# VectorE's chain of the stick-breaking branch, from the maximum on, in pieces of one head, each tied to a weight split

## The chip, the cores and the metric

One core of a Trainium2 chip runs the whole program; the other cores are idle. The metric is the time of one execution on the device in microseconds (us), and lower is better. TensorE (PE; its weight loads are PEld) does the matmuls, VectorE (DVE), ScalarE (ACT) and GpSimd (POOL) the rest, and SyncE (SP) issues nearly all loads. Each engine takes its instructions in the order in which the program lists them.

## The reference, cut to what matters

Two layers; in each, four token mixers (a, b, c, d) share one input projection, each has a gate, and a merge adds the four with per-channel gates. The change is in branch d, stick-breaking attention with 4 heads of 64 and a sequence of 512:

```python
z = jnp.einsum('bqhd,bkhd->bhqk', qblk, k).astype(jnp.float32) * scale
mask = kpos[None, :] < t[:, None]
log1m = jnp.where(mask, jax.nn.log_sigmoid(-z), 0.0)
after = lax.cumsum(log1m, axis=3, reverse=True) - log1m
a = jnp.where(mask, jnp.exp(jax.nn.log_sigmoid(z) + after), 0.0)
return jnp.einsum('bhqk,bkhd->bqhd', a.astype(v.dtype), v)
...
for i, y in enumerate((y_a, y_b, y_c, y_d)):
    gate = jax.nn.sigmoid(h @ w_merge[l, i] + b_merge[l, i])
    merged = merged + gate * (y @ w_branch[l, i])
```

## The kernel before

**Matmuls in three passes.** Every large product is made of three fp32r matmuls of 128x512 (`mm3`, L195 to L197): the high part of one operand with the high part of the other, high with low, and low with high. So each weight that is loaded must first be split.

**Weight chunks.** `split_chunk` loads one 128-column chunk of a weight into a `stage` buffer (three of them), ScalarE (L184) and GpSimd (L102) round its high part, and one VectorE subtraction (L186) makes the low part. The first matmul of a chunk waits for L186. High and low parts live in four buffers `w5`, that is two chunks, so the rounding of a chunk can begin only when TensorE has read the chunk before the last for the last time. A merge chunk (`merge_chunks`) has 24 matmuls on the shared input `hT` and 6 on a branch's output `y`; then ScalarE takes a Tanh (L395), VectorE multiplies and adds (L400, L402), and GpSimd accumulates (L403).

**Branch d.** Its 4 heads are worked in two chains of 2 heads, `pr` 0 and 1, in each layer: four chains in all. The scores of the four query blocks (128, 256, 384 and 512 wide) of both heads are packed into three tiles, `ze[0][0..2]`: the first two (tag `x4`) are 128 x 2 heads x 512, the third (tag `su`) 128 x 2 x 256. The first holds query block 3, the second blocks 1 and 2, the third block 0 and nothing else of weight. For the three tiles in turn VectorE takes min (L757) and ScalarE Exp and Ln(1+.) (L758, L761). Then, tile by tile, VectorE takes the maximum with z (L767), runs reversed prefix sums in place (L775, one scan for each query block and head), and subtracts (L776), and ScalarE takes Exp (L777). `pv_cluster` transposes the result (L332), copies it (L334) and multiplies it with v (L339); `finish_pair` (L347 to L349) applies the gate.

**What sets the order.** The program is written down once; a scheduler in the framework then orders the instructions of each engine by priorities and its own estimate of time. `high_priority` puts branch work ahead of the merge chunks around it, so that the chunks fill TensorE while a branch waits for its softmax. `after(first, then, ...)` adds a dependency by hand. Two of these concern the chain: each Ln waits for the rounding of a certain chunk (`w_round`), and the maximum of tiles 0 and 1 waits for the low part of a certain chunk (`w_split`), so that the split goes first on VectorE:

```python
larger = V.tensor_tensor(ze[1][j], ze[0][j], ze[1][j], op=OP.max)
if j < 2:
    after(w_split[(n_10 + 1, n_11 + 3)[pr] + j], larger, "weights first")
```

`n_10` and `n_11` are the numbers of the first chunk of two stretches of the merge. In the rows of the first layer, chain 0 runs beside the chunks `w_450/451`, `w_457/458` (that is `n_11`) and `w_463/464`, chain 1 beside `w_476/477`, `w_480/481`, `w_486/487` and the two after them, `w_710/711` and `w_716/717` (after the change the first number of a name is the same or a little higher in the later ones). The even or odd larger number of a pair is the low part, which L186 writes. At the end of branch c stand the chunks `w_809/810`, `w_815/816` and `w_823/824`.

Of the kernel before, what the change touches and what calls it, by code (L numbers as in the profile page):

```python
# [12 lines left out]
AF = mybir.ActivationFunctionType  # L13
OP = mybir.AluOpType
# [74 lines left out]
def hybrid_trunk(ctx: ExitStack, tc: tile.TileContext, x, norm_g, w_in, mla_q_norm, mla_w_uq, mla_kv_norm,  # L89
# [3 lines left out]
    V, A, G, T = nc.vector, nc.scalar, nc.gpsimd, nc.tensor  # L93
# [55 lines left out]
    def ps_o():  # L149
        return mk(ps, [P, 512], F32, "po", 1)  # L150
# [37 lines left out]
    def after(first, then, why):  # L188

        tc.add_manual_dep(then.ins, first.ins.name, mybir.DependencyInfo(  # L190
            mybir.DependencyClass.Sync, mybir.DependencyReason.DATA), reason=why)
# [49 lines left out]
    w_round, w_split = [], []  # L241
# [209 lines left out]
    for l in range(DEPTH):  # L451
# [274 lines left out]
        n_10 = len(w_split)  # L726
# [8 lines left out]
        n_11 = len(w_split)  # L735
# [5 lines left out]
        with tc.high_priority(offset=tc.cur_priority - mark):  # L741
            y[3] = new_y()
            for pr in range(2):
                ze = [(x4([P, 2, 512]), x4([P, 2, 512]), unit_tile().rearrange("p (h c) -> p h c", h=2)) for _ in range(2)]
                place = ((1, 384, 512), (2, 0, 256), (1, 0, 384), (0, 0, 512))

                def part(i, qt, h):
                    j, c0, c1 = place[qt]
                    return ze[i][j][:, h, c0:c1]

                for qt in (3, 2, 0, 1):
                    w = (qt + 1) * P
                    for h in range(2):
                        s = qk_unit(stacked(d_q[pr], d_k[pr][h], h), qt, w)
                        V.tensor_tensor(part(0, qt, h), s[:, :w], mask_tab[:, S + 1 - w:], op=OP.subtract)
                for j in range(3):
                    V.tensor_scalar(ze[1][j], ze[0][j], 30.0, None, op0=OP.min)  # L757
                    ex = A.activation(ze[1][j], ze[1][j], AF.Exp)  # L758
                with tc.issue_after(ex.ins):
                    for j in range(3):  # L760
                        ln = A.activation(ze[1][j], ze[1][j], AF.Ln, bias=1.0)  # L761

                        after(w_round[(n_10 + 1, n_11 + 2)[pr]], ln, "weights first")
                        if pr == 0:
                            after(ln, gelu, "one table at a time")
                for j in range(3):
                    larger = V.tensor_tensor(ze[1][j], ze[0][j], ze[1][j], op=OP.max)  # L767
                    if j < 2:

                        after(w_split[(n_10 + 1, n_11 + 3)[pr] + j], larger, "weights first")  # L770
                    for qt in range(NT):
                        if place[qt][0] == j:
                            for h in range(2):
                                er = part(1, qt, h)[:, ::-1]
                                V.tensor_tensor_scan(er, er, er, 0.0, op0=OP.add, op1=OP.bypass)  # L775
                    V.tensor_tensor(ze[0][j], ze[0][j], ze[1][j], op=OP.subtract)  # L776
                    A.activation(ze[0][j], ze[0][j], AF.Exp)  # L777
                acc = ps_o()
                for qts in ((3,), (2,), (0, 1)):
                    pv_cluster([([part(0, qt, h) for h in range(2)], qt,  # L780
                                 lambda h, kb: v_ad[1][:, kb, (2 * pr + h) * 64:(2 * pr + h + 1) * 64], False, True)
                                for qt in qts], acc)
                d_done = finish_pair(acc, gd, y[3], pr)
# [130 lines left out]
```

## Time and profile before

| | |
|---|---|
| median of 3 runs | 1095.86 us (1093.76 to 1097.98) |
| the profiled execution, its own time | 1093.13 us |
| its span, first to last instruction | 1091.4 us |
| TensorE busy in the span | 1068.1 us (98%) |
| VectorE / ScalarE / GpSimd busy | 592.9 us (54%) / 440.0 us (40%) / 251.4 us (23%) |
| granted TensorE clock, mean | 0.998 of full speed (2.4 GHz is 1) |

The span lies within the execution's own time; 1.7 us lie around it. A row of the timeline has the start in us from the span's start, the time that it takes, the engine, the source line and operation, output and inputs, and in brackets how long the engine was idle before and on what it waited. Several instructions of a line in a row are one row (x2, x8). The end of a matmul is modelled: matmuls of 128x512 follow each other some 0.23 us apart though each is listed with 0.39.

### The profile page before, as it was taken

How to read it: one execution, taken by the hardware profiler on the slowest of the kernel's cores; microseconds unless marked ns; L12 is line 12 of the kernel's file. 1: busy time of each engine (PE TensorE's matmuls, PEld its weight loads, DVE VectorE, ACT ScalarE, POOL GpSimd, SP SyncE). 2: the span in 40 equal slices, each digit the busy share in tenths (PEclk: the TensorE clock that was granted, in tenths of full speed). 3: DMA queues.
4: the chain of work that ended last, by engine and by line, in shares of the span. 5: the costliest groups of instructions: out<-in, count | busy, mean ns of one | idle time of the engine just before them, and what ended most of it. 6: DMA issues, size and time to landing. Idle time of an engine off the chain costs nothing.

```text
span 1091.4 us, 15131 instructions
## 1 busy us (share of the span) xinstructions
PE 1068.1 (98%) x5652; PEld 858.8 (79%) x5652; DVE 592.9 (54%) x1136; ACT 440.0 (40%) x894; POOL 251.4 (23%) x270
## 2 busy tenths in 40 slices
PE   8999999999999999999999999999999999999997
PEld 6888887877778878788888888778787888777886
DVE  6435565568645646355443565466857455563542
ACT  5424343454433535233243343434545334352322
POOL 3221020202133132342011311111023222323321
PEclk9999999999999999999999999999999999999999
DMA  8423252422232212246313323443132322213412
GB/s 249 105 58 78 65 152 64 141 73 78 73 87 82 74 54 68 87 124 191 103 39 98 79 77 88 117 126 102 44 97 75 95 73 68 78 49 113 139 58 77
DMA packets 161676, 100.86 MB, mean 92 GB/s; under 512 B 14913, under 2 KB 151489, under 8 KB 161602
## 3 DMA queue, kind: packets, MB, share of 16 engines
q1 hardware_dynamic: 160880, 98.75, 31.6%
q8 instruction: 44, 0.72, 0.3%
q10 hardware_dynamic: 722, 1.14, 0.3%
q14 instruction: 30, 0.25, 0.1%
HBM read 95.67 MB, written 4.19 MB: 92 GB/s over the span
## 4 chain that ended last, share of the span: by engine, by line
PE 88%; DVE 6%; DMA 2%; ACT 2%; issue 1%; SPq 0%; POOL 0%; POOLq 0%; DVEq 0%; ACTq 0%
PE pd L195 24%; PE pd L196 23%; PE pd L197 23%; PE po L339 5%; PE pss L302 4%; PE pt L332 4%; DMA stage<-in_w_out_dram 2%; DVE w L186 2%; DVE x L775 2%; PE pt L692 1%; ACT w L184 0%; DVE su L775 0%; DVE s L551 0%; DMA stage<-in_w_in_dram 0%; PE pd L643 0%
## 5 line engine op out<-in xcount | busy, mean ns | idle before, releaser
L195 PE MATMUL pd<-hT,w 128*128 128x512 f32 x832 | 333.7, 401 | 8.4 <-DVE w L186 8.2
L197 PE MATMUL pd<-hT,w 128*128 128x512 f32 x832 | 331.9, 399 | 0.0
L196 PE MATMUL pd<-hT,w 128*128 128x512 f32 x832 | 331.5, 398 | 0.0
L102 POOL TENSOR_SCALAR w<-stage 128x640 fp32r<-128x640 f32 (+1 forms) x104 | 72.3, 696 | 617.9 <-PE pd L196 316.6
L195 PEld LDWEIGHTS pd<-hT,w 128*128 128x128 f32 x832 | 156.5, 188 | 46.8 <-DVE w L186 11.5
L186 DVE TENSOR_TENSOR w<-stage,w 128x1280 fp32r<-128x1280 f32 (+1 forms) x104 | 145.4, 1398 | 83.5 <-ACT w L184 51.4
L197 PEld LDWEIGHTS pd<-hT,w 128*128 128x128 f32 x832 | 156.5, 188 | 35.2 <-issue 1.1
L196 PEld LDWEIGHTS pd<-hT,w 128*128 128x128 f32 x832 | 156.5, 188 | 33.4 <-issue 0.3
L403 POOL TENSOR_TENSOR s<-s,th 128x512 f32<-128x512 f32 x48 | 111.0, 2313 | 62.3 <-DVE th L402 59.2
L184 ACT ACTIVATE w<-stage 128x640 fp32r<-128x640 f32 x104 | 76.5, 736 | 88.8 <-PE pd L196 77.9
L314 ACT ACTIVATE su<-su,stat 128x128 f32<-128x128 f32 (+3 forms) x128 | 71.2, 557 | 76.5 <-DVE stat L312 76.4
L334 ACT ACTIVATE pt<-pt 128x384 f32<-128x384 f32 (+2 forms) x120 | 59.4, 521 | 96.0 <-PE pt L332 95.2
L395 ACT ACTIVATE th<-pd,bmT 128x512 f32<-128x512 f32 x64 | 43.9, 686 | 104.3 <-PE pd L197 104.0
L402 DVE SCALAR_TENSOR_TENSOR th<-th,pd 128x512 f32<-128x512 f32 x48 | 32.8, 684 | 75.1 <-PE pd L197 75.0
L332 PE MATMUL pt<-small,su 128*128 128x128 f32 x336 | 57.7, 279 | 1.5 <-DVE su L317 1.5
L195 PE MATMUL pd<-y,w 128*128 128x512 f32 x128 | 51.4, 404 | 0.3
L332 PEld LDWEIGHTS pt<-small,su 128*128 128x128 f32 x336 | 39.8, 140 | 14.4 <-issue 6.2
L197 PE MATMUL pd<-y,w 128*128 128x512 f32 x128 | 50.5, 395 | 0.0
L196 PE MATMUL pd<-y,w 128*128 128x512 f32 x128 | 50.4, 394 | 0.0
L312 DVE CUSTOM_DVE_ANT_0 su<-pss,dist_tab 128x128 f32<-128x128 f32 (+3 forms) x64 | 28.9, 486 | 37.8 <-PE pss L302 37.8
L196 PE MATMUL pd<-y,hT 128*128 128x512 f32 (+1 forms) x112 | 44.1, 397 | 0.0
L195 PE MATMUL pd<-y,hT 128*128 128x512 f32 (+1 forms) x112 | 43.4, 396 | 0.0
(251 smaller groups left out, 1540.6 us busy)
## 6 DMA issues: line engine op xcount, KB each, us to landing
stage<-in_w_merge_dram SPq DMA_DIRECT2D x64, 512.0 KB, 3.9
stage<-in_w_in_dram SPq DMA_DIRECT2D x38, 512.0 KB, 3.9
stage<-in_w_branch_dram SPq DMA_DIRECT2D x64, 128.0 KB, 3.8
stage<-in_w_out_dram SPq DMA_DIRECT2D x16, 512.0 KB, 4.1
stage<-in_w_in_dram SPq DMA_DIRECT2D x20, 256.0 KB, 3.8
x<-in_nsa_w_dram SPq DMA_DIRECT2D x8, 512.0 KB, 4.9
stage<-in_w_in_dram SPq DMA_DIRECT2D x8, 352.0 KB, 4.6
x<-in_tab_a_dram SPq DMA_DIRECT2D x4, 512.0 KB, 4.4
```

The source lines that it names most:

```text
L102: G.tensor_scalar(o, i, 1.0, 1.0, op0=OP.mult, op1=OP.mult)
L184: r = A.activation(hi[:, :a], src[:, :a], AF.Copy)
L186: return r, V.tensor_tensor(lo, src, hi.bitcast(F32), op=OP.subtract)
L195: first = T.matmul(acc, sh, mh, start=start, stop=False)
L196: T.matmul(acc, sh, ml, start=False, stop=False)
L197: T.matmul(acc, sl, mh, start=False, stop=stop)
L314: A.activation(e[:, :width], e[:, :width], AF.Exp, scale=-1.0, bias=st[:, 0:1], accum_out=st[:, 1:2])
L332: T.transpose(pt[:, i], u[0][h][:, kb * P:(kb + 1) * P], ident)
L334: ready = A.activation(pT[:, :n], pt[:, :n], AF.Copy)
L339: pv = T.matmul(acc[64 * h:64 * h + 64, qt * P:(qt + 1) * P], v(h, kb), pTs[h][:, i], start=(kb == 0 and not started), stop=(kb == qt and ...
L395: A.activation(th, pg, AF.Tanh, scale=0.5, bias=bmT[l][:, 8 * i + c:8 * i + c + 1])
L403: G.tensor_tensor(acc[:, j], acc[:, j], th, op=OP.add)
```

## The change

The loop over three tiles becomes a loop over five pieces: head 0 and head 1 of the first tile, head 0 and head 1 of the second, and the third tile whole. Each piece has its own maximum, its own scans (those of its query blocks and head), its own subtraction and its own Exp. Each maximum is tied to the split of a chunk: the pieces to the chunks 0, 1, 1, 2, 2 counted from `w_split[n_10 + 1]` in chain 0 and from `w_split[n_11 + 3]` in chain 1.

```diff
-                for j in range(3):
-                    larger = V.tensor_tensor(ze[1][j], ze[0][j], ze[1][j], op=OP.max)
-                    if j < 2:
-                        after(w_split[(n_10 + 1, n_11 + 3)[pr] + j], larger, "weights first")
+                for j, h, chunk in ((0, 0, 0), (0, 1, 1), (1, 0, 1), (1, 1, 2), (2, None, 2)):
+                    hs = slice(None) if h is None else h
+                    z, e = ze[0][j][:, hs], ze[1][j][:, hs]
+                    larger = V.tensor_tensor(e, z, e, op=OP.max)
+                    after(w_split[(n_10 + 1, n_11 + 3)[pr] + chunk], larger, "weights first")
                     for qt in range(NT):
                         if place[qt][0] == j:
-                            for h in range(2):
-                                er = part(1, qt, h)[:, ::-1]
+                            for h_ in range(2) if h is None else (h,):
+                                er = part(1, qt, h_)[:, ::-1]
                                 V.tensor_tensor_scan(er, er, er, 0.0, op0=OP.add, op1=OP.bypass)
-                    V.tensor_tensor(ze[0][j], ze[0][j], ze[1][j], op=OP.subtract)
-                    A.activation(ze[0][j], ze[0][j], AF.Exp)
+                    V.tensor_tensor(z, z, e, op=OP.subtract)
+                    A.activation(z, z, AF.Exp)
```

In the changed program the maximum is L770, the scan L776, the subtraction L777 and the Exp L778.

**First place: VectorE in chain 0** of the first layer, from the first maximum on (`x_493`, `x_494`, `su_2530` are z in the three tiles, `x_496`, `x_497`, `su_2533` the tiles that are summed). Before:

```order
L767 TENSOR_TENSOR x_496_2531<-x_493_2528,x_496_2531 128x1024
L767 TENSOR_TENSOR x_497_2532<-x_494_2529,x_497_2532 128x1024
L767 TENSOR_TENSOR su_2533<-su_2530,su_2533 128x512
L658 TENSOR_SCALAR gelu_2017<-gelu_2017 128x64
L775 SCALAR_TENSOR_TENSOR x_496_2531<-x_496_2531 128x512 x2
L775 SCALAR_TENSOR_TENSOR x_497_2532<-x_497_2532 128x128 x2
L775 SCALAR_TENSOR_TENSOR x_497_2532<-x_497_2532 128x384 x2
L775 SCALAR_TENSOR_TENSOR su_2533<-su_2533 128x256 x2
L659 TENSOR_TENSOR hid_1972<-gelu_2017,hid_1972 128x64
L400 SCALAR_TENSOR_TENSOR s_442_2189<-th_2266,pd_2268 128x512
L186 TENSOR_TENSOR w_464_2327<-stage_2323,w_463_2326 128x1280
```

Of the change, behind the two maxima of the first tile (one row, L770 x2):

```order
L770 TENSOR_TENSOR x_497_2532<-x_494_2529,x_497_2532 128x512
L776 SCALAR_TENSOR_TENSOR x_496_2531<-x_496_2531 128x512
L658 TENSOR_SCALAR gelu_2017<-gelu_2017 128x64
L776 SCALAR_TENSOR_TENSOR x_496_2531<-x_496_2531 128x512
L776 SCALAR_TENSOR_TENSOR x_497_2532<-x_497_2532 128x128
L776 SCALAR_TENSOR_TENSOR x_497_2532<-x_497_2532 128x384
L777 TENSOR_TENSOR x_493_2528<-x_493_2528,x_496_2531 128x512
L659 TENSOR_TENSOR hid_1972<-gelu_2017,hid_1972 128x64
L777 TENSOR_TENSOR x_493_2528<-x_493_2528,x_496_2531 128x512
L400 SCALAR_TENSOR_TENSOR s_442_2189<-th_2266,pd_2268 128x512
L777 TENSOR_TENSOR x_494_2529<-x_494_2529,x_497_2532 128x512
L186 TENSOR_TENSOR w_464_2327<-stage_2323,w_463_2326 128x1280
```

The second half of the second tile and the whole third tile (two maxima, four scans) now stand behind the split of `w_464`, and three subtractions of 512 columns stand ahead of it that stood behind.

**Second place: VectorE and ScalarE in chain 1** of the first layer (`x_521`, `x_522`, `su_2657` or `su_2663` are z; `x_524`, `x_525`, `su_2660` or `su_2666` the tiles that are summed). VectorE before:

```order
L402 SCALAR_TENSOR_TENSOR th_2471<-th_2471,pd_2473 128x512
L767 TENSOR_TENSOR x_524_2658<-x_521_2655,x_524_2658 128x1024
L767 TENSOR_TENSOR x_525_2659<-x_522_2656,x_525_2659 128x1024
L775 SCALAR_TENSOR_TENSOR x_524_2658<-x_524_2658 128x512 x2
L186 TENSOR_TENSOR w_711_3357<-stage_3353,w_710_3356 128x1280
```

VectorE in the change:

```order
L770 TENSOR_TENSOR x_524_2664<-x_521_2661,x_524_2664 128x512 x2
L776 SCALAR_TENSOR_TENSOR x_524_2664<-x_524_2664 128x512
L770 TENSOR_TENSOR x_525_2665<-x_522_2662,x_525_2665 128x512 x2
L776 SCALAR_TENSOR_TENSOR x_524_2664<-x_524_2664 128x512
L402 SCALAR_TENSOR_TENSOR th_2471<-th_2471,pd_2473 128x512
L777 TENSOR_TENSOR x_521_2661<-x_521_2661,x_524_2664 128x512
L770 TENSOR_TENSOR su_2666<-su_2663,su_2666 128x512
L776 SCALAR_TENSOR_TENSOR x_525_2665<-x_525_2665 128x128
L776 SCALAR_TENSOR_TENSOR x_525_2665<-x_525_2665 128x384
L186 TENSOR_TENSOR w_711_3369<-stage_3365,w_710_3368 128x1280
```

L402, a subtraction, the third tile's maximum and two scans have moved ahead of the split of `w_711`. ScalarE at the same place before (the Tanh of `th_2471` stood just ahead of these rows):

```order
L758 ACTIVATE su_2660<-su_2660 128x512
L761 ACT_TABLE_LOAD
L761 ACTIVATE x_524_2658<-x_524_2658 128x1024
L761 ACTIVATE x_525_2659<-x_525_2659 128x1024
L184 ACTIVATE w_710_3356<-stage_3353 128x640
L761 ACTIVATE su_2660<-su_2660 128x512
L395 ACT_TABLE_LOAD
L395 ACTIVATE th_2515<-pd_2490,bmT_263 128x512
L184 ACTIVATE w_716_3399<-stage_3396 128x640
```

ScalarE in the change:

```order
L758 ACTIVATE su_2666<-su_2666 128x512
L761 ACT_TABLE_LOAD
L761 ACTIVATE x_524_2664<-x_524_2664 128x1024
L761 ACTIVATE x_525_2665<-x_525_2665 128x1024
L395 ACT_TABLE_LOAD
L395 ACTIVATE th_2471<-pd_2446,bmT_263 128x512
L761 ACT_TABLE_LOAD
L761 ACTIVATE su_2666<-su_2666 128x512
L184 ACTIVATE w_710_3368<-stage_3365 128x640
L778 ACT_TABLE_LOAD
L778 ACTIVATE x_521_2661<-x_521_2661 128x512
```

A table is loaded four times instead of twice here (for Ln, Tanh, Ln, Exp), the Tanh of `th_2471` stands between the Ln of the first two tiles and that of the third, and the rounding of `w_710` stands behind all three Ln. Chain 1 of the second layer is the same; in the whole program there are 13 such loads instead of 9. On TensorE eight transposes of this chain (L332) stood behind the last matmul of `w_710`; now four stand ahead of its first matmul, and seven, three of them of the second tile, among its last ones. The last multiplication with v of chain 0 (L339) stands three matmuls of 128x512 earlier.

**Third place: the end of branch c**, in both layers (`y_558`, `y_559` are the two parts of the branch's output). VectorE before:

```order
L186 TENSOR_TENSOR w_816_4106<-stage_4102,w_815_4105 128x1280
L347 SCALAR_TENSOR_TENSOR su_3348<-po_3086,s_468_2367 128x512
L349 TENSOR_TENSOR y_559_2819<-su_3348,y_558_2818 128x512
L402 SCALAR_TENSOR_TENSOR th_4089<-th_4089,pd_4091 128x512
L186 TENSOR_TENSOR w_824_4154<-stage_4150,w_823_4153 128x1280
L402 SCALAR_TENSOR_TENSOR th_4135<-th_4135,pd_4137 128x512
```

VectorE in the change:

```order
L186 TENSOR_TENSOR w_816_4118<-stage_4114,w_815_4117 128x1280
L347 SCALAR_TENSOR_TENSOR su_3360<-po_3098,s_468_2367 128x512
L349 TENSOR_TENSOR y_559_2831<-su_3360,y_558_2830 128x512
L402 SCALAR_TENSOR_TENSOR th_4101<-th_4101,pd_4103 128x512
L402 SCALAR_TENSOR_TENSOR th_4147<-th_4147,pd_4149 128x512
L186 TENSOR_TENSOR w_824_4166<-stage_4162,w_823_4165 128x1280
L186 TENSOR_TENSOR w_830_4212<-stage_4208,w_829_4211 128x1280
```

TensorE before, up to the first matmul of `w_823`:

```order
L195 MATMUL pd_4137<-y_558_2818,w_815_4105 128x512
L196 MATMUL pd_4091<-y_559_2819,w_809_4059 128x512
L197 MATMUL pd_4091<-y_558_2818,w_810_4060 128x512
L196 MATMUL pd_4137<-y_559_2819,w_815_4105 128x512
L197 MATMUL pd_4137<-y_558_2818,w_816_4106 128x512
L195 MATMUL pd_4137<-y_558_2818,w_815_4105 128x512
L196 MATMUL pd_4137<-y_559_2819,w_815_4105 128x512
L197 MATMUL pd_4137<-y_558_2818,w_816_4106 128x512
L195 MATMUL pd_4158<-hT_75,w_823_4153 128x512
```

TensorE in the change:

```order
L195 MATMUL pd_4149<-y_558_2830,w_815_4117 128x512
L196 MATMUL pd_4149<-y_559_2831,w_815_4117 128x512
L197 MATMUL pd_4149<-y_558_2830,w_816_4118 128x512
L195 MATMUL pd_4103<-y_558_2830,w_809_4071 128x512
L195 MATMUL pd_4149<-y_558_2830,w_815_4117 128x512
L196 MATMUL pd_4103<-y_559_2831,w_809_4071 128x512
L197 MATMUL pd_4103<-y_558_2830,w_810_4072 128x512
L196 MATMUL pd_4149<-y_559_2831,w_815_4117 128x512
L197 MATMUL pd_4149<-y_558_2830,w_816_4118 128x512
L195 MATMUL pd_4170<-hT_75,w_823_4165 128x512
```

The last use of `w_810` stands three matmuls later against the first matmul of `w_823`, and both L402 stand ahead of the split of `w_824`, where one stood behind it. On SP and on GpSimd nothing moves at the first two places; one load (L604, `w2v`) is issued a place earlier.

## Rows read from the trace of the kernel before

**Rows 1.** The page, part 1: busy us, share of the span and instructions of each engine.

```profile
PE 1068.1 (98%) x5652; PEld 858.8 (79%) x5652; DVE 592.9 (54%) x1136; ACT 440.0 (40%) x894; POOL 251.4 (23%) x270
```

**Rows 2.** The page, part 4: the chain that ended last, shares by engine.

```profile
PE 88%; DVE 6%; DMA 2%; ACT 2%; issue 1%; SPq 0%; POOL 0%; POOLq 0%; DVEq 0%; ACTq 0%
```

**Rows 3.** Waits of TensorE: waited for, us in total, times, longest us.

```profile
PE pd L195 <- DVE w L186: 8.2, 8, 1.6
...
PE pt L332 <- DVE su L317: 1.5, 4, 0.4
PE po L339 <- ACT pt L334: 1.2, 2, 0.6
```

**Rows 4.** Timeline of TensorE, chain 0 of the first layer, and its twin.

```profile
253.06 0.31 PE L661 MATMUL pt<-hid,w2k 128*128 128x32 f32 x2
254.98 0.50 PE L195 MATMUL pd<-hT,w 128*128 128x512 f32 x1 [1.61 <-DVE w L186]
...
790.67 0.50 PE L195 MATMUL pd<-hT,w 128*128 128x512 f32 x1 [1.61 <-DVE w L186]
```

**Rows 5.** Timeline of VectorE, chain 0 of the first layer.

```profile
243.07 2.36 DVE L767 TENSOR_TENSOR x<-x,x 128x1024 f32<-128x1024 f32 x2 [0.53 <-ACT x L761]
245.35 0.68 DVE L767 TENSOR_TENSOR su<-su,su 128x512 f32<-128x512 f32 x1
246.11 0.75 DVE L658 TENSOR_SCALAR gelu<-gelu 128x64 f32<-128x64 f32 x1
246.78 4.65 DVE L775 TENSOR_TENSOR_SCAN x<-x 128x512 f32<-128x512 f32 x6
251.35 1.24 DVE L775 TENSOR_TENSOR_SCAN su<-su 128x256 f32<-128x256 f32 x2
...
252.74 0.69 DVE L400 SCALAR_TENSOR_TENSOR s<-th,pd 128x512 f32<-128x512 f32 x1
253.35 1.58 DVE L186 TENSOR_TENSOR w<-stage,w 128x1280 fp32r<-128x1280 f32 x1
```

**Rows 6.** Timeline of ScalarE, rounding of `w_463`.

```profile
246.69 0.73 ACT L184 ACTIVATE w<-stage 128x640 fp32r<-128x640 f32 x1
```

**Rows 7.** Timeline of TensorE, chain 1 of the first layer.

```profile
295.95 0.50 PE L195 MATMUL pd<-hT,w 128*128 128x512 f32 x1
...
303.02 1.03 PE L332 MATMUL pt<-small,x 128*128 128x128 f32 x8
304.85 0.50 PE L195 MATMUL pd<-hT,w 128*128 128x512 f32 x1 [0.80 <-DVE w L186]
```

**Rows 8.** Timeline of ScalarE, chain 1.

```profile
286.29 0.69 ACT L395 ACTIVATE th<-pd,bmT 128x512 f32<-128x512 f32 x1 [0.28 <-PE pd L197]
286.88 0.62 ACT L758 ACTIVATE su<-su 128x512 f32<-128x512 f32 x1
287.52 1.28 ACT L761 ACT_TABLE_LOAD   x1
288.81 2.01 ACT L761 ACTIVATE x<-x 128x1024 f32<-128x1024 f32 x2
```

**Rows 9.** Timeline of VectorE, chain 1.

```profile
289.90 2.36 DVE L767 TENSOR_TENSOR x<-x,x 128x1024 f32<-128x1024 f32 x2 [1.55 <-ACT x L761]
292.18 2.33 DVE L775 TENSOR_TENSOR_SCAN x<-x 128x512 f32<-128x512 f32 x2
294.43 1.47 DVE L186 TENSOR_TENSOR w<-stage,w 128x1280 fp32r<-128x1280 f32 x1
```

**Rows 10.** Timelines of TensorE and VectorE, end of branch c, first layer.

```profile
461.45 0.39 PE L197 MATMUL pd<-y,w 128*128 128x512 f32 x1
463.07 0.50 PE L195 MATMUL pd<-hT,w 128*128 128x512 f32 x1 [1.23 <-DVE w L186]
...
460.75 0.69 DVE L402 SCALAR_TENSOR_TENSOR th<-th,pd 128x512 f32<-128x512 f32 x1 [5.22 <-PE pd L197]
461.52 1.49 DVE L186 TENSOR_TENSOR w<-stage,w 128x1280 fp32r<-128x1280 f32 x1
```

## Prediction

> **What bounds the kernel now.** I read the page's busy shares first: TensorE is busy 98% of the span, VectorE 54%, ScalarE 40%, GpSimd 23% [rows 1]. The chain that ended last lies on TensorE for 88% [rows 2]. So a step on VectorE or ScalarE costs or gives time only where TensorE stands still for it. The third view is therefore TensorE's waits. The largest item is 8.2 us in 8 waits for the low part of a weight chunk (L186 on VectorE); the waits of branch a, which runs beside branch c, make 1.5 and 1.2 us [rows 3]. The change cuts VectorE's chain, in which some of those splits stand, so it can give back part of 8.2 us, or add to it. Neither is large beside 1093 us.
>
> The profiled execution took 1093.13 us, 2.7 under the median of 1095.86. The sum is made against 1093.13, and 2.7 is added at the end. Some 0.5%, or 5.5 us, is what a measurement of this kernel can tell from no change.
>
> **Prices.** Starts that follow each other give what an instruction costs in a busy queue. Two maxima of 128x1024 start at 243.07 and the next instruction at 245.35, so 1.14 each; a tensor operation of 512 columns takes 0.60 to the next start (L400, 252.74 to 253.35) [rows 5]. A scan of 512 takes 1.13 (two from 292.18 to 294.43) [rows 9]; six scans take 4.57 (246.78 to 251.35), so a 128 and a 384 together 1.16, and two of 256 take 1.17 [rows 5]. A maximum or subtraction cut in two thus costs 1.20 where it cost 1.14. A table load on ScalarE takes 1.28, and an operation of 512 columns 0.62 [rows 8]. Matmuls of 128x512 come 0.23 apart.
>
> **Place 1, chain 0, the split of `w_464`.** Before, VectorE begins the maxima at 243.07 and comes to L186 at 253.35 [rows 5]. TensorE is done with what stands ahead at 253.06 + 0.31 = 253.37, and begins the chunk at 254.98 after 1.61 us of idling, 1.63 after L186 began; the second layer shows 1.61 again [rows 4]. In the change half of the second maximum (0.54), the third maximum (0.60) with the short idling behind it (0.08), two scans of 128 and 384 (1.16) and the two of the third tile (1.17) move behind L186: 3.55 less. Ahead of it come one more cut (0.06) and three subtractions of 512 (1.80): 1.86 more. L186 begins 1.69 earlier, at 251.66, and the chunk could begin at 253.29, about when TensorE is free. ScalarE rounds its half of `w_463` from 246.69 for 0.73 [rows 6], so the split's input is long there. I take the whole wait of 1.6, in two layers: **-3.2**. The lower bound is 1.0 a layer, if each of some six cut pieces costs 0.1 more than its row says. The first subtraction's Exp can start earlier too, but the chain ends behind later chunks, so I count nothing for it.
>
> One rule of the Trainium skill speaks against this place: "VectorE: DVE Perf Modes", section "The TRN2 errata — SBUF-src ops pay a fixed extra latency per instruction", has every VectorE operation from SBUF carry a fixed cost, and a fp32 tensor operation of N columns take (N+151)/0.96 ns, an estimate of 0.69 us for 512. The listed durations agree with it, 0.68 for 512 and 1.22 for 1024 (2.36 less 1.14) [rows 5], but in a busy queue the starts lie 0.60 apart, so most of the fixed part overlaps the neighbour's. By the rule six tensor operations ahead of each split would cost 0.5 more at both this place and the next, and the sum below would be about 2 us higher; I go by the starts.
>
> **Place 2, chain 1, the split of `w_711`.** Before, the first maximum begins at 289.90 behind the Ln, and L186 at 294.43 [rows 9]; the chunk follows at 295.95, without a wait [rows 7]. ScalarE's Tanh of 286.29, ahead of which it idled for 0.28, moves behind the Ln, so that the first of these rows could come 0.87 earlier (0.28 + 0.59) [rows 8]; and the last multiplication with v of chain 0 stands three matmuls (0.7) earlier, which the rows ahead of it wait for. Between 0.87 and 1.57 I take 1.1: load from 286.42, Ln to 289.72, first maximum at 288.80. Ahead of L186 come, beside the 4.53 of before (289.90 to 294.43), an L402 (0.60), a subtraction (0.60), the third maximum (0.60), two scans (1.16) and two cuts (0.12): 7.61. So L186 begins at 296.41, and the chunk 1.52 later (295.95 less 294.43 [rows 7, 9]) at 297.93, **1.98 late**. What makes the third maximum late is ScalarE: behind the Ln of the first two tiles it loads for Tanh (1.28), takes the Tanh (0.69), loads for Ln again (1.28) and takes the Ln (0.62), from 289.72 to about 293.55; VectorE comes to that maximum at 288.80 + 5.88 = 294.68. That is 1.1 us of slack.
>
> Not all of 1.98 stays. The next chunk, `w_716`, waited 0.80 for its split at 304.85, behind eight transposes of 1.03 [rows 7]. In the change four transposes stand inside the new wait and cost nothing, seven (0.9) stand at the end of `w_710`. TensorE comes to `w_716` at 297.93 + 7.07 (295.95 to 303.02) + 0.9 = 305.9. VectorE comes to the split of `w_717` at 296.41 + 1.39 + 1.16 + 0.60 + 1.17 + 0.60 + 0.60 = 301.9, before it is needed, so that wait is gone. 305.9 less 304.85 is 1.05; three of the seven transposes (0.39) would otherwise have come later. So 0.65 a layer: **+1.3**. Bounds: nothing, if the chain starts 1.57 earlier and the rest of the delay goes into later waits, and 2.0, if nothing is given back.
>
> **Place 3, the end of branch c, the split of `w_824`.** Before, TensorE's last matmul of `w_815` begins at 461.45 and the next chunk at 463.07 after 1.23 of idling; L402 began at 460.75, when the last use of `w_810` was done, and L186 at 461.52 [rows 10]. Now that last use comes three matmuls (0.69) later, and two L402 (0.60 each, one more than before) stand ahead of the split, the second of them behind the last matmul of the group. L186 begins at about 462.64, and the chunk at 464.2: +1.1 a layer, **+2.2**. Bounds: nothing, if the scheduler's order hides it, and 1.2. This has nothing to do with branch d: it is what the scheduler makes of other numbers.
>
> **The rest.** Between chain 1 and place 3 rows of branches a and c change places by one or two. There is no wait there now but branch a's 2.7 us in both layers [rows 3]. I take nothing; the bounds are nothing and 2.7 once more. SP and GpSimd have the same work in the same order at places 1 and 2.
>
> **The sum**: -3.2 + 1.3 + 2.2 = +0.3, so 1093.4 for a profiled execution, and with 2.7 a median of **1096.2**. The ends are -3.2 and -2.0 + 4.0 + 2.4 + 2.7 = +7.1, so 1092.6 to 1102.9 as medians.
>
> **Rivals.**
> A, slower: ScalarE's switches of tables cost more than their rows. The place is place 2: past 1.1 us of slack each further us delays the third maximum, and with it the split of `w_711` and TensorE. If each of three loads there costs as much again (1.28), the delay is 3.84 less 1.1 = 2.7 a layer, +5.5 in two: 1101.7. Against it speaks that the load of 287.52 takes 1.28 and the Ln begins at 288.81, at once behind it [rows 8]. The Trainium skill, "ScalarE: Activation LUTs", section "What ACT_TABLE_LOAD costs", adds some 1.38 us of draining to a load of 1.28, 2.66 for every switch; by it the time would be some 0.6 above this rival's. The row ahead of the load, of 0.62, ends as the load begins, which doesn't show such a drain. Chance 0.08.
>
> B: the split of `w_464` gains nothing, since each piece waits for the one before it (a scan for its maximum, a subtraction for its scan, in a chain that runs dry). Some 0.28 for each of six links makes up the 1.69. Then +3.5: 1099.4. Against it: in the pieces of before, scan behind scan, the starts show no such gap, though each maximum had two others between itself and its scan [rows 5]. Chance 0.15.
>
> C: places 2 and 3 cost nothing, because ScalarE starts earlier than I take it and the order at branch c only shifts a wait. Then -3.2: 1092.7. Chance 0.15.
>
> My forecast, that places 2 and 3 give back what place 1 gains, has 0.54; 0.08 is left for what I don't see.
>
> **How the numbers follow.** Range: the bounds give 1092.6 to 1102.9; a median of three runs spreads by 2 us, and I leave out the highest part, where all bounds meet: 1091 to 1102. Faster by over 0.5% means under 1090.4, below even rival C: 0.06. Slower means over 1101.3: most of A, and some of the rest, 0.11. Same: 0.83.
>
> **What would show it.** In the profile after: no wait of TensorE at the first matmul of `w_463`, near 253.3 and its twin; a wait of about 2 us for L186 at `w_710` near 296 to 298, and none at `w_716`; a wait of some 2.3 us at the end of branch c in place of 1.23; thus 8.2 us of waits for L186 again, spread otherwise; four loads of a table in each chain 1, each followed at once by its operation. I am wrong if the wait of 1.61 remains, if the third maximum of chain 1 waits for ScalarE, or if a wait appears elsewhere.

## The result and the profile after

The changed kernel took 1104.64 us (median of 7, 1100.65 to 1105.39), the kernel before 1095.30 beside it (1092.58 to 1097.98): a ratio of 1.0077 with an interval of 1.0061 to 1.0093, **slower by 9.3 us**. The forecast was no change, 1096.2, with a range to 1102. The profiled execution has a span of 1102.8 us where before it was 1091.4, 11.4 more. This is the page, part 1, of the changed kernel, beside [rows 1]:

```profile
PE 1075.5 (98%) x5652; PEld 862.8 (78%) x5652; DVE 599.6 (54%) x1152; ACT 446.3 (40%) x906; POOL 248.2 (23%) x270
```

TensorE is busy 7.4 us longer with the same 5652 matmuls. That is the first sign of something that the forecast has no term for: not waiting, but slower matmuls. The waits of TensorE (us in total, times, longest), beside [rows 3]:

```profile
PE pd L195 <- DVE w L186: 10.8, 6, 2.5
...
PE pss L302 <- DVE x L755: 1.1, 4, 0.3
...
PE pt L332 <- ACT x L778: 0.7, 2, 0.4
```

The wait for L186 is up by 2.6 us in sum, in 6 waits and not 8, the longest 2.5. Of the small ones beside it, that of the softmax transposes for the first Exp (L778) is new, and that for L755 has two more. At place 1 TensorE now goes on without a wait, where it stood for 1.61 [rows 4]; the second layer is the same:

```profile
251.30 0.30 PE L661 MATMUL pt<-hid,w2k 128*128 128x32 f32 x2
...
252.91 0.47 PE L195 MATMUL pd<-hT,w 128*128 128x512 f32 x1
```

At place 2, chain 1, the timeline of TensorE shows three things: a wait of 0.35 for the first Exp, four transposes, and a wait of 2.51 for the split of `w_711`, where before there was none [rows 7]. Between 294.6 and 298.1 TensorE runs only those transposes. From the fifth matmul or so of the chunk on, starts lie 0.43 apart and not 0.23:

```profile
294.24 0.39 PE L197 MATMUL pd<-y,w 128*128 128x512 f32 x1
294.98 0.65 PE L332 MATMUL pt<-small,x 128*128 128x128 f32 x4 [0.35 <-ACT x L778]
298.14 0.50 PE L195 MATMUL pd<-hT,w 128*128 128x512 f32 x1 [2.51 <-DVE w L186]
...
298.94 0.48 PE L195 MATMUL pd<-hT,w 128*128 128x512 f32 x1
299.22 0.63 PE L196 MATMUL pd<-hT,w 128*128 128x512 f32 x1
...
301.78 0.63 PE L196 MATMUL pd<-hT,w 128*128 128x512 f32 x1
...
302.59 0.40 PE L195 MATMUL pd<-hT,w 128*128 128x512 f32 x1
```

The windows show it as the granted clock. The columns are the length, PE, PEld, DVE, ACT and POOL busy time with their instruction counts, then the clock, the DMA share and GB/s:

```profile
296.00:298.00 2.00, 0.00 (x0) 0.00 (x0) 2.00 (x2) 0.61 (x2) 0.75 (x1) 1.00 0.00 0
298.00:300.00 2.00, 1.86 (x6) 1.52 (x7) 2.00 (x5) 0.11 (x1) 0.00 (x0) 0.78 0.31 90
300.00:302.00 2.00, 2.00 (x6) 1.53 (x5) 2.00 (x4) 0.86 (x2) 0.00 (x0) 0.50 0.81 238
302.00:304.00 2.00, 2.00 (x9) 1.58 (x9) 2.00 (x3) 0.29 (x1) 1.70 (x1) 0.87 0.00 0
```

The clock falls from 1.00 to 0.50, that is from 2.4 to 1.2 GHz, behind TensorE's longest pause, and comes back by 302.6. VectorE and GpSimd in the same stretch:

```profile
287.48 1.29 DVE L770 TENSOR_TENSOR x<-x,x 128x512 f32<-128x512 f32 x2 [2.47 <-ACT x L761]
...
293.33 0.68 DVE L770 TENSOR_TENSOR su<-su,su 128x512 f32<-128x512 f32 x1
293.93 2.30 DVE L776 TENSOR_TENSOR_SCAN x<-x 128x128 f32<-128x128 f32 x2
296.15 1.93 DVE L186 TENSOR_TENSOR w<-stage,w 128x1280 fp32r<-128x1280 f32 x1
298.01 1.26 DVE L776 TENSOR_TENSOR_SCAN x<-x 128x128 f32<-128x128 f32 x2
```

```profile
292.89 2.52 POOL L403 TENSOR_TENSOR s<-s,th 128x512 f32<-128x512 f32 x1 [6.08 <-DVE th L402]
295.38 1.37 POOL L102 TENSOR_SCALAR w<-stage 128x640 fp32r<-128x640 f32 x1
```

VectorE comes to the third maximum at 293.33 without idling, so ScalarE's additional loads do not delay it. But the pair of scans behind it takes 2.30 and the same pair behind the split 1.26, and L186 takes 1.93 where it took 1.47 [rows 9]. Each time GpSimd is at work: on the addition L403 in the first case, on the rounding of `w_716` in the second. At place 3 a wait of 2.37 stands for 1.23 [rows 10], with seven slow matmuls from there on:

```profile
463.70 0.39 PE L197 MATMUL pd<-y,w 128*128 128x512 f32 x1
466.46 0.79 PE L195 MATMUL pd<-hT,w 128*128 128x512 f32 x1 [2.37 <-DVE w L186]
...
469.19 0.63 PE L195 MATMUL pd<-hT,w 128*128 128x512 f32 x1
```

**The bill.** Starts of the same matmul, after less before, put the loss in place. At 238 us the change is 0.37 ahead (237.80 against 238.17, a difference of the start); at a matmul of the output projection at the end of the layer, L195 on `s`, it is 4.88 behind (518.20 against 513.32). So a first layer costs 5.25, and the second with the end 6.6. In the whole execution 35 matmuls run at 0.43 (7 behind `w_710` and 7 behind `w_823` in the first layer, 14 and 7 in the second): 35 times 0.20 is **7.0 us of clock**. The rest, some 4.8 from 238 us on, I put down to waiting, 2.4 a layer: place 1 gives 1.6 back, place 3 takes 1.14 and a small new wait 0.26, so that 2.6 is left for place 2, as a remainder.

### The profile page after: what moved, and what is told of

It is laid out like the page before. It is cut to its first block, busy times and chain, and to the rows that moved or that the text cites. A ratio compares the mean times of both kernels' runs of the same rounds, so it can differ in the third digit from the quotient of the medians.

```text
span 1102.8 us, 15145 instructions
## 1 busy us (share of the span) xinstructions
PE 1075.5 (98%) x5652; PEld 862.8 (78%) x5652; DVE 599.6 (54%) x1152; ACT 446.3 (40%) x906; POOL 248.2 (23%) x270
## 3 DMA queue, kind: packets, MB, share of 16 engines
q10 hardware_dynamic: 722, 1.14, 0.3%
## 4 chain that ended last, share of the span: by engine, by line
PE 84%; DVE 7%; issue 3%; ACT 3%; DMA 2%; POOL 0%; SPq 0%; POOLq 0%; DVEq 0%; ACTq 0%
PE pd L195 23%; PE pd L196 23%; PE pd L197 23%; PE po L339 4%; PE pss L302 4%; PE pt L332 4%; DVE w L186 2%; DMA stage<-in_w_out_dram 1%; DVE x L776 1%; ACT L761 1%; PE pt L692 1%; ACT w L184 1%; DMA x<-in_x_dram 0%; DVE x L770 0%; DVE x L777 0%
## 5 line engine op out<-in xcount | busy, mean ns | idle before, releaser
L195 PE MATMUL pd<-hT,w 128*128 128x512 f32 x832 | 337.0, 405 | 11.0 <-DVE w L186 10.8
L195 PEld LDWEIGHTS pd<-hT,w 128*128 128x128 f32 x832 | 158.5, 191 | 49.5 <-DVE w L186 13.4
L186 DVE TENSOR_TENSOR w<-stage,w 128x1280 fp32r<-128x1280 f32 (+1 forms) x104 | 151.7, 1460 | 81.4 <-ACT w L184 51.7
L197 PEld LDWEIGHTS pd<-hT,w 128*128 128x128 f32 x832 | 158.3, 190 | 34.8 <-issue 0.4
L196 PEld LDWEIGHTS pd<-hT,w 128*128 128x128 f32 x832 | 158.4, 190 | 34.0 <-issue 0.5
L403 POOL TENSOR_TENSOR s<-s,th 128x512 f32<-128x512 f32 x48 | 107.5, 2242 | 68.6 <-DVE th L402 63.2
L402 DVE SCALAR_TENSOR_TENSOR th<-th,pd 128x512 f32<-128x512 f32 x48 | 32.6, 683 | 84.4 <-PE pd L197 83.9
L332 PE MATMUL pt<-small,su 128*128 128x128 f32 x336 | 57.6, 279 | 1.5 <-DVE su L317 1.5
L332 PEld LDWEIGHTS pt<-small,su 128*128 128x128 f32 x336 | 39.9, 140 | 14.2 <-issue 5.9
L195 PE MATMUL pd<-y,w 128*128 128x512 f32 x128 | 50.7, 401 | 0.3
L195 PE MATMUL pd<-y,hT 128*128 128x512 f32 (+1 forms) x112 | 43.4, 397 | 0.0
```

The lines of the kernel that those rows point to most:

```text
L186: return r, V.tensor_tensor(lo, src, hi.bitcast(F32), op=OP.subtract)
L195: first = T.matmul(acc, sh, mh, start=start, stop=False)
L196: T.matmul(acc, sh, ml, start=False, stop=False)
L197: T.matmul(acc, sl, mh, start=False, stop=stop)
L332: T.transpose(pt[:, i], u[0][h][:, kb * P:(kb + 1) * P], ident)
L403: G.tensor_tensor(acc[:, j], acc[:, j], th, op=OP.add)
```

## The experiments

My theory was then: (1) the clock falls behind the longest waits, and costs more than they do; (2) VectorE's scans and splits are slowed by GpSimd instructions that the new order puts beside them; (3) what makes chain 1 late is the order that the scheduler chose, not the pieces. The rivals: the waits alone are the loss; the pieces of chain 1 cost by themselves; table loads. Each run is compared with the kernel before on the same chip, three chips in all: 1096.02 beside the runs 1, 2, 5 and the first of 3, 1094.88 beside those of 4, the second of 3 and the first of 6, 1094.39 beside the last three. Where a run is set against the change, the two were not timed together; the kernel before differs by up to 0.9 us from the 1095.30 beside the change, and by up to 1.6 between the runs. Line numbers of the experiments differ from the change's by a few. None of them leaves out work.

**1. TensorE kept busy in the waits.** Ten matmuls on `hT` alone, whose result the next `start` overwrites:

```diff
         hi, lo, done = w
+        for k in range(fill):
+            T.matmul(acc, hT[0][:, 0, :P], hT[0][:, k % KD], start=True, stop=True)
...
-                proj_T(w, pg)
+                proj_T(w, pg, {(2, 0, 0): 10, (1, 2, 0): 10}.get((cp, i, j), 0))
```

> The changed kernel, with ten more matmuls of 128x512 on hT alone, whose result is overwritten, ahead of the first matmul of w_710 and of w_823 in both layers; VectorE's order up to those places stays. Theory (the clock): the waits of 2.5 and 2.4 us for L186 stay as late in time, but TensorE works through them, so the granted clock stays at 1.00 behind them, and the 8 to 14 matmuls that took 0.43 each take 0.23 again: 1.8 and 2.8 us back at w_710, 1.45 twice at w_823, about 7.5 in all, so about 1097 us. Rival (the waits alone are the loss, the clock falls for another reason or costs nothing): within 1 us of the changed kernel, 1104.

Measured: 1095.98, 8.7 us under the change, ratio to before 1.000 (0.9978 to 1.0022). TensorE, then the window that was at 0.50:

```profile
294.57 2.46 PE L261 MATMUL pd<-hT 128*128 128x512 f32 x10
...
298.26 0.50 PE L195 MATMUL pd<-hT,w 128*128 128x512 f32 x1 [0.33 <-DVE w L186]
298.60 0.40 PE L196 MATMUL pd<-hT,w 128*128 128x512 f32 x1
```

```profile
300.00:302.00 2.00, 2.00 (x13) 1.64 (x11) 2.00 (x4) 1.34 (x3) 0.00 (x0) 1.00 0.85 249
```

The chunk begins at 298.26, as late as in the change (298.14), and its matmuls now come 0.23 apart. With the arrival unchanged, what came back at place 2 is the clock. The scheduler also put two matmuls of each of these chunks on `y` ahead of the wait, 0.46 at each of four places, or 1.9 us; so of 8.7 some 6.8 are the clock's, beside 7.0 in the bill. The first layer, where no fall is left in this run, checks the other part of the bill: from 237.90 to 514.38 it takes 1.33 more than before, and 2.2 with the 0.9 of moved matmuls added, where the bill has 2.4 of waiting.

Two things are not as expected. At `w_823` the scheduler put the split ahead of the second L402 again, as before the change, so only place 2 tests the clock with the arrival unchanged. And the clock fell once elsewhere, in branch a of the second layer, where no wait is over 0.58 and TensorE ran little but transposes and narrow matmuls between three short waits:

```profile
714.46 0.88 PE L341 MATMUL po<-pt,s 128*64 128x128 f32 x12 [0.58 <-ACT pt L336]
715.26 0.65 PE L195 MATMUL pd<-hT,w 128*128 128x512 f32 x1
```

So a fall does not need one long wait. Doing useless work was worth more than the whole change was meant to give.

**2. GpSimd's addition taken away from the scans**, by one dependency:

```diff
         merge_chunks(l, MERGE_REST, y, am, mT)
+        after(w_split[n_rest], gate_op[l, 0, 0, 0][1], "no addition beside the scans")
```

(`n_rest` is the number of `w_710`'s chunk, `gate_op` holds L402 and L403 of each merge chunk.)

> The changed kernel, with GpSimd's addition of th_2471 (L403) bound behind the split of w_711 in both layers, nothing else moved. Theory (contention): the 128 and 384 scans ahead of that split took 2.2 us beside L403 where such a pair takes 1.16, and L186 1.93 beside the late rounding of w_716 where it takes 1.49; without L403 there the split ends 1.5 us earlier, the wait at w_710 falls from 2.5 to about 1.0, the clock stays up there, so 1.5 + 1.8 and 1.5 + 2.8 us come back: about 1097. Rival (the scans are slow for another reason): scans and wait as in the changed kernel, 1104.

Measured: 1099.38, ratio 1.0027 (1.0007 to 1.0048), 5.3 under the change. VectorE and GpSimd:

```profile
295.61 1.27 DVE L779 TENSOR_TENSOR_SCAN x<-x 128x128 f32<-128x128 f32 x2
296.79 1.94 DVE L186 TENSOR_TENSOR w<-stage,w 128x1280 fp32r<-128x1280 f32 x1
298.65 2.31 DVE L779 TENSOR_TENSOR_SCAN x<-x 128x128 f32<-128x128 f32 x2
```

```profile
296.16 1.24 POOL L102 TENSOR_SCALAR w<-stage 128x640 fp32r<-128x640 f32 x1 [7.66 <-PE pd L196]
298.81 1.34 POOL L405 TENSOR_TENSOR s<-s,th 128x512 f32<-128x512 f32 x1 [1.42 <-DVE w L186]
```

The pair of scans ahead of the split takes 1.27 again. The slow pair, 2.31, is now the one behind the split, where L403 has gone: the slowness moves with the addition. So it is shown that the two engines hold each other up here. L186 still takes 1.94, beside the rounding of 296.16, which I had thought would be over by then. The wait at `w_710` fell to 1.49 and not to 1.0. The clock stayed up there in the first layer and fell in the second, so less came back than I expected.

**3. The end of branch c, two attempts.** First only the second L402 behind the split:

```diff
+        after(w_split[gate_op[l, 1, 2, 0][2]], gate_op[l, 0, 2, 1][0], "split first")
```

> The changed kernel, with the second L402 at the end of branch c bound behind the split of w_824 in both layers, nothing else moved. Theory: the split begins 0.6 us earlier, the wait falls from 2.37 to about 1.75, the clock does not fall there, 0.6 + 1.45 us a layer come back: about 1100.5. Rival (it costs 0.6 a layer and the clock falls all the same): 1103.4.

Measured: 1103.29, ratio 1.0064 (1.0043 to 1.0085). The split of the change, then the split of this run and the matmul behind it:

```profile
464.88 1.53 DVE L186 TENSOR_TENSOR w<-stage,w 128x1280 fp32r<-128x1280 f32 x1
```

```profile
462.43 1.99 DVE L186 TENSOR_TENSOR w<-stage,w 128x1280 fp32r<-128x1280 f32 x1
```

```profile
464.48 0.50 PE L195 MATMUL pd<-hT,w 128*128 128x512 f32 x1 [2.37 <-DVE w L186]
```

The split starts 0.47 earlier against TensorE (462.43 less 461.72, the start of the last matmul ahead of the wait, for 464.88 less 463.70) and takes 0.46 longer, and the wait is 2.37 as in the change. Taking VectorE's second L402 away alone gains nothing. In the changed order GpSimd rounds `w_829` right behind `w_823` (before the change an addition stood between), and the split, which now starts earlier, runs beside that rounding. The second attempt binds it too (`pool_round` holds GpSimd's roundings):

```diff
+        after(w_split[gate_op[l, 1, 2, 0][2]], pool_round[gate_op[l, 1, 2, 0][2] + 1], "no rounding beside the split")
```

> The change, with the second L402 at the end of branch c and GpSimd's rounding of w_829 both bound behind the split of w_824. Theory (the split is slow beside the rounding of the next chunk: 1.99 us in place of 1.49): it takes 1.49 again, the wait at w_823 falls from 2.37 to about 1.9, and the clock falls there more rarely: 1101 to 1103.5. Rival (GpSimd's rounding doesn't matter): split 1.99 and wait 2.37 as in the run that moved L402 alone, 1103 to 1104.5.

Measured: 1099.59, ratio 1.0052 (1.0035 to 1.0070):

```profile
463.01 1.49 DVE L186 TENSOR_TENSOR w<-stage,w 128x1280 fp32r<-128x1280 f32 x1
```

```profile
464.56 0.50 PE L195 MATMUL pd<-hT,w 128*128 128x512 f32 x1 [1.87 <-DVE w L186]
```

1.49 and 1.87, as the theory said. The median is below what was expected; in the profiled execution the clock does not fall at this place in either layer, where it fell in both in the change. (In both attempts the profiled execution is the fastest of eleven, so this says little of the others.)

**4. Which chain does it.** Pieces in chain 0 alone, then (with `pr == 1` in the condition) in chain 1 alone, the other in whole tiles, whose third maximum is bound to no chunk:

```diff
-                for j, h, chunk in ((0, 0, 0), (0, 1, 1), (1, 0, 1), (1, 1, 2), (2, None, 2)):
+                for j, h, chunk in (((0, 0, 0), (0, 1, 1), (1, 0, 1), (1, 1, 2), (2, None, 2)) if pr == 0 else ((0, None, 0), (1, None, 1), (2, None, None))):
```

> Pieces and their bindings in chain 0 alone; chain 1 in whole tiles, its first two maxima bound as before. The scheduler still puts the Tanh of th_2471 (and its L402, L403) inside chain 1 and the third tile and four scans ahead of the split of w_711, and the tail of branch c as in the change. Theory (the harm in chain 1 comes from the order that the gain of chain 0 sets off, not from the pieces): place 1 keeps its 1.6 a layer, the wait at w_710 is 2.5 to 3.2 us again with a fall of the clock in most executions, the wait at w_823 2.37: as slow as the change, 1103 to 1106. Rival (the pieces of chain 1 make the wait): the wait at w_710 is under 1 us, about 1097.

> Pieces in chain 1 alone; chain 0 in whole tiles. Here the split of w_711 stands behind four half maxima and two scans, and the Tanh ahead of the Ln, as before the change. Theory: the wait of 1.61 at w_463 stays, w_710 begins without a wait, the wait at w_823 is 2.37 for 1.23, and the clock falls behind it in some executions: 1097.5 to 1100.5. Rival (pieces in chain 1 are what costs): a wait over 2 us at w_710 and 1102 or more.

Measured: chain 0 alone 1105.02, ratio 1.0091 (1.0069 to 1.0114); chain 1 alone 1098.60, ratio 1.0025 (1.0009 to 1.0042). TensorE with pieces in chain 0 alone, at `w_710`:

```profile
299.41 0.50 PE L195 MATMUL pd<-hT,w 128*128 128x512 f32 x1 [4.01 <-DVE w L186]
```

And in chain 1 alone, at `w_463`, `w_716` and `w_823`:

```profile
254.02 0.50 PE L195 MATMUL pd<-hT,w 128*128 128x512 f32 x1 [1.61 <-DVE w L186]
...
303.51 0.50 PE L195 MATMUL pd<-hT,w 128*128 128x512 f32 x1 [0.26 <-DVE w L186]
...
462.88 0.50 PE L195 MATMUL pd<-hT,w 128*128 128x512 f32 x1 [2.37 <-DVE w L186]
```

With no piece in chain 1 the wait at its chunk is 4.01, longer than in the change; with pieces there alone it is none. So at this place the pieces of chain 1 do no harm: the order does. With chain 0 cut, whether or not chain 1 is cut, the Tanh of `th_2471` stands behind the Ln of chain 1 and the third tile stands ahead of `w_711`; with chain 1 alone cut they stand as before. The end of branch c is changed in both, and with chain 1 alone cut the loss that the waits show lies there (2.37 for 1.23).

**5. The split of `w_711` first.** The scans of the second tile and the third maximum bound behind it:

```diff
+        for late in behind:
+            after(w_split[n_rest], late, "weights first")
```

> The changed kernel, with the scans of the second tile and the third maximum of chain 1 bound behind the split of w_711 in both layers, so that this split begins behind the first subtraction. The scheduler then also puts the split of w_824 ahead of the second L402. Theory: the split of w_711 begins about 2.8 us earlier, so about 2.6 of the wait at w_710 and the 1.8 and 2.8 us at half clock come back, and at w_823 0.6 + 1.45 a layer: about 1091, faster than the kernel before by the 3.2 us of the first place and little else. Rival (the later third tile moves the wait on to w_716 or to the transposes of this chain): waits of 1 to 2 us there, 1095 to 1098.

Measured: 1097.56, ratio 1.0017 (0.9997 to 1.0038), 7.1 under the change but 6 over the theory:

```profile
303.50 0.50 PE L195 MATMUL pd<-hT,w 128*128 128x512 f32 x1 [0.27 <-DVE w L186]
...
308.20 0.33 PE L332 MATMUL pt<-small,x 128*128 128x128 f32 x1 [0.83 <-ACT pt L334]
...
463.37 0.50 PE L195 MATMUL pd<-hT,w 128*128 128x512 f32 x1 [2.14 <-DVE w L186]
```

No wait for the split of `w_711` is left, but the later third tile makes new ones (0.27, 0.83), and the split of `w_824` still runs beside the roundings, with a wait of 2.14. The time is the rival's; the new waits are smaller than its 1 to 2 us.

**6. A bound order with the pieces.** One dependency, the Ln of chain 1 behind the Tanh of `th_2471`, puts the split of `w_711` ahead of the whole chain; with it the two bindings of attempt two (`gate_th` holds the Tanh of each merge chunk):

```diff
                         if pr == 0:
                             after(ln, gelu, "one table at a time")
+                        else:
+                            after(gate_th[l, 0, 0, 0], ln, "one table at a time")
```

> All pieces; in chain 1 the Ln bound behind the Tanh of th_2471, by which the scheduler puts the split of w_711 ahead of the whole chain; at the end of branch c the second L402 and the rounding of w_829 behind the split of w_824. Theory: place 1 gives 3.2 us, no wait at w_710, 1.9 at w_823 for 1.23 (1.3 in two layers), no fall of the clock in most executions: about 2 us under the kernel before of the same call. Rival (chain 1, now behind the split, is late for w_716 and the transposes): waits of 1 us there, within 1 us of the kernel before.

Measured: 1093.48, ratio 0.9988 (0.9974 to 1.0003), not clear of no change; at `w_716` and `w_823`:

```profile
302.93 0.50 PE L195 MATMUL pd<-hT,w 128*128 128x512 f32 x1 [0.70 <-DVE w L186]
...
461.73 0.50 PE L195 MATMUL pd<-hT,w 128*128 128x512 f32 x1 [1.87 <-DVE w L186]
```

Another version orders TensorE too (`f`, the first matmul of `w_815` on `y`, behind `before`, the last one of `w_809/810`):

```diff
+                    if (cp, i, j, k) == (0, 2, 1, 0):
+                        after(before, f, "the older chunk first")
```

> The version with the Ln bound behind the Tanh and the second L402 and the rounding of w_829 behind the split of w_824 (1093.5 in its call), with the matmuls of w_815 on y bound behind the last one of w_809/810 in TensorE's order, so that the older chunk is read for the last time six matmuls before the wait and not two. Theory: the rounding of w_823 starts 0.9 us earlier, the wait at w_823 falls from 1.87 to about 0.95, 0.9 a layer comes back: about 3.5 us under the kernel before of this call. Rival (rounding or stage buffer is released by something else): wait 1.87, as the version without it.

Measured: 1092.73, ratio 0.9984 (0.9976 to 0.9993). At place 3 the wait is 1.00 in the first layer, as expected, and 2.13 in the second. VectorE's split and GpSimd's addition in either layer tell why:

```profile
460.54 1.49 DVE L186 TENSOR_TENSOR w<-stage,w 128x1280 fp32r<-128x1280 f32 x1
...
995.32 2.62 DVE L186 TENSOR_TENSOR w<-stage,w 128x1280 fp32r<-128x1280 f32 x1
```

```profile
460.54 2.64 POOL L414 TENSOR_TENSOR s<-s,th 128x512 f32<-128x512 f32 x1
...
995.31 1.28 POOL L414 TENSOR_TENSOR s<-s,th 128x512 f32<-128x512 f32 x1
```

In the first layer the split takes 1.49 and the addition 2.64; in the second the addition takes 1.28 and the split 2.62. They take turns: 1.49 and 1.28 make 2.77, a little more than the one behind takes. In both layers the two starts lie within 0.01 us, so the rows do not tell which will be first.

Last, pieces in chain 0 alone with the bindings of the first of these versions, and no pieces at all with those of the second, the one on TensorE among them:

> Pieces in chain 0 alone, with the Ln of chain 1 bound behind the Tanh of th_2471, and the two bindings at the end of branch c. The order at w_711 and at the end of branch c is then that of the kernel before, but for the four scans and both subtractions of chain 1, which stand behind its maxima. Theory: the 3.2 us of place 1 remain, 1.23 at w_823 as before, and w_716 waits up to 1.5 for its split: 1.5 to 3.5 us under the kernel before of this call. Rival (the pieces of chain 1 are needed for w_716): a wait of over 2 there and no gain.

> The kernel before, whole tiles in both chains, with the bindings of the other runs (Ln behind Tanh, second L402 and rounding behind the split, the matmuls of w_815 behind w_809/810). It already has that order but for one matmul on TensorE, so it tells what the bindings are worth without the pieces. Theory (the gain of the bound version comes from the pieces at place 1): waits of 1.61 at w_463 and about 1.0 at w_823, 0.2 to 0.5 us under the kernel before. Rival (the bindings alone are the gain): 2 us or more under it.

Measured: chain 0 alone **1091.72, ratio 0.9975 (0.9965 to 0.9985)**, 2.7 us under the kernel before and the fastest of all; no pieces 1096.05, ratio 1.0021 (1.0008 to 1.0034). With chain 0 alone, at `w_716` and `w_823`:

```profile
303.36 0.50 PE L195 MATMUL pd<-hT,w 128*128 128x512 f32 x1 [1.03 <-DVE w L186]
...
461.57 0.50 PE L195 MATMUL pd<-hT,w 128*128 128x512 f32 x1 [1.23 <-DVE w L186]
```

The three bindings alone lose: one matmul moved at the end of branch c lets the addition start ahead of the split there, with a wait of 2.13 for 1.23 in both layers. That is 1.8 of the 4.3 us between these two; what is left is place 1, where the version without pieces waits 1.61 twice, less small waits elsewhere. In the profiled execution without pieces the clock also falls behind the first 2.13. So the pieces of chain 0 gain. Those of chain 1 show no gain: with them and the same bindings the ratio was 0.9988, and the intervals overlap. Whole tiles with only the bindings of the Ln and of VectorE and GpSimd at branch c were not run.

## Why the prediction was wrong, point by point

- **Place 1** was right: the wait is gone in both layers, at 252.91 for a forecast near 253.3, 0.37 of it being the start. The version above keeps it. Rival B is refuted.
- **Place 2** was right in kind and too small; here the sum failed first. The forecast had the chunk 1.98 late; measured against a TensorE and a chain that both come earlier by place 1's gain and the start (1.97), it is 2.2 later still. Three pieces make that up. I took 1.1 for the Ln's earlier start and got 0.45 (the first maximum at 287.48, that is 289.90 less 1.97 less 0.45): 0.65. The scans beside L403 took 2.22 to the next start for 1.16: 1.06. The split beside the rounding took 0.46 more. The step that failed was the price list: I took a row's duration as a property of the instruction, and moved L402 without asking where its L403 on GpSimd goes. The order on record showed L402 ahead of those scans, and the trace of before showed elsewhere, in the second layer, what a split costs beside that addition:

```profile
959.36 2.62 DVE L186 TENSOR_TENSOR w<-stage,w 128x1280 fp32r<-128x1280 f32 x1
...
959.34 1.28 POOL L403 TENSOR_TENSOR s<-s,th 128x512 f32<-128x512 f32 x1
```

- **Place 3** was right, in size (1.14 for 1.1) and in its rows: from the start of the last matmul ahead of the wait, the split comes 1.18 later and the chunk 2.76 (464.88 and 466.46 less 463.70), for a forecast of 1.19 and 2.75. What the forecast did not have is a second limit as near: without the second L402 the split meets the rounding of `w_829` and ends no sooner. With both bound 0.50 of the 1.14 is gone; the rest goes with the later last reading of `w_810`, since ordering TensorE there too took the wait to 1.00 in the first layer.
- **The clock** was the term that I didn't have, and the largest: 7.0 of 11.4 us in the profiled execution. The second step that failed is that I priced a wait at its own length and the slowdown behind it at nothing. In the trace of before no wait behind the start is over 1.61 us, and no fall follows one in these stretches; that should have stood as a warning that a wait longer than any shown has no price in the rows. By the run that filled the waits the change without it costs some 2 us by the medians (1095.98 and the 1.9 of moved matmuls, beside 1096.02) and some 4.5 by the trace, an estimate (2.2 in the first layer, twice); either is within my range. Two of the 34 executions of the kernel before beside that run took 1104, with a mean granted clock of 0.993, so in some its clock falls too.
- **Rival A** did not come about: the third maximum has no idle time ahead of it. The wait of 0.35 for the first Exp, behind the fourth load, lies ahead of the wait for the split, which comes last. **Rival C** fell with the two places that it had at nothing.
- **The range** ended at 1102, and its untrimmed end at 1102.9, because its upper bounds were sums of waits.

## What to carry to other kernels

A gain early in a program changes the order that a scheduler makes later; compare orders far behind the edit, on GpSimd too, and price each moved instruction together with what depends on it. A duration read from a trace holds for the neighbours that it had there: ask what the other engine does at the new place. And a wait of TensorE that is made longer than any in the trace may cost up to its length again in slow matmuls, so bind the order, or give TensorE something to do.

## What the runs showed that I had not expected

**VectorE and GpSimd take turns.** A subtraction or scan of VectorE with both operands in SBUF, on-chip memory that both engines use, took up to its own time and that of a GpSimd instruction beside it, and GpSimd's up to its own and VectorE's: scans of 128 and 384 together took 1.26 and 2.30, the split 1.49 and 2.62, GpSimd's addition 1.28 and 2.64. L402, which has one operand in PSUM (the memory that TensorE writes to), took 0.66 to 0.69 everywhere. The Trainium skill, "SBUF — State Buffer", section "SBUF: two separate sides", says that the two engines arbitrate for one port pair, an exclusive lock, in which a VectorE instruction with two SBUF inputs or a GpSimd instruction, whichever starts first, has the pair to its end and the other blocks. The traces agree that one blocks the other. That the one that starts first has the pair does not show in the rows' starts: in the change L403 is listed from 292.89, and the maximum of 293.33 behind it takes its usual 0.68.

**The clock does not fall each time.** Over the kernels' profiled executions, of the waits for L186 of 2.1 to 2.5 us 11 of 21 were followed by matmuls at half speed, both of 4.0, and 1 of 16 of those of 1.2 to 1.9 (the 1.49 in the run that moved the addition). In the run that moved the second L402, waits of 2.52 and 2.37 passed without a fall, and 2.51 did not. Behind these falls 7 to 14 matmuls of 128x512 ran at the slow pace. The seven times of the change lie in two groups, and the mean granted clock of each execution goes with them: 0.996 for the three of 1100.65 to 1101.17, 0.991 or 0.992 for the four of 1104.64 to 1105.39, among them the profiled one. So the bill is that of the four.
